# A mixture-of-experts loop on one Trainium2 core: rows taken from a table in memory, weight splits on one engine, a branch hint moved

## The chip, the core and the metric

The kernel runs on one core of a Trainium2 chip, in one launch. Its engines are TensorE (PE, matmuls into PSUM), VectorE (DVE), ScalarE (ACT), GpSimd (POOL) and SyncE (SP). Here SP issues nearly all plain DMA transfers and POOL the indirect ones, which gather or scatter rows by a list of row numbers in SBUF. Each engine runs its own list of instructions in order, and engines wait for each other on semaphores. The metric is the device time of one execution in microseconds; lower is better.

## What is computed

One layer of a hybrid decoder over 1024 tokens of width 1024, in float32: a LayerNorm, one wide projection, three token mixers (gated DeltaNet, mLSTM, latent attention), their gated merge and output projection, a LayerNorm, a mixture of 16 experts with top-2 routing inside one of four groups, and a last LayerNorm. The change touches the experts:

```python
def routed_experts(x, router_w, router_bias, w1, w3, w2):
    expert, weight = route(x_flat, router_w, router_bias)
    ...
    def expert_ffn(args):
        xb, e = args
        return (jax.nn.silu(xb @ w1[e]) * (xb @ w3[e])) @ w2[e]
    ...
    out = jnp.zeros((n_tok, d), x.dtype).at[row_tok].add((y_rows * row_w[:, None]).astype(x.dtype))
```

So each expert needs the numbers of the tokens sent to it, their weights, and their rows of x.

## The kernel before

**Stages.** The first 1382 us are everything up to the second LayerNorm. Then the router scores all tokens (`route_choose`, `route_weights`), and `experts` runs the 16 experts one after another. Each token's place within its expert's list stands in `posx` (tokens on partitions, one column an expert).

**How an expert's rows are found.** `mark(e)` makes eight one-hot tiles on VectorE (L1437) that compare `posx` with 0 to 255. `find(e)` multiplies them with `aux` (token number, a valid flag, the weight in three bfloat16 parts) on TensorE (L1455), which leaves the list by place; `found(e)` spreads the further places over quarters of rows (four matmuls, L1461) and makes, in some dozen small VectorE operations (L1464 to L1480), `idx` (which row to gather, which row of the result to add to) and the weights `wsl`. Both have four buffers.

**One expert.** Places 0 to 127 are a full block: `fetch(e)` gathers the 128 rows of 4 KB into `xg` (POOL, L1489); `turn_a` transposes them on TensorE (`pxg`, L1505) and splits them into a high and a low part (`xgH` on ScalarE, `xgL` on VectorE); `layer1` multiplies with w1 and w3 in eight chunks c (`ph`, L1535), `act` makes silu times gate (`mhh`), `turn2` transposes (`phT`, L1510) and `layer2` multiplies with w2 in four chunks (`py`). The result is scaled by the weights on ScalarE (`mo`, L1743) and added to its rows of `x1r` in memory by an indirect DMA of POOL (L1494). Places from 128 on are up to four parts of 32, each under a branch on the expert's count; they gather quarter rows into `xm`, run in `part_x`, `part_1`, `part_act`, `part_h`, `part_2`, `part_y` on the tile `bank`, and end in `mom` and up to four more adds. The branch code stands at the helper line L1659; `ahead` places a hint that names a later branch of TensorE.

**Weights.** Each weight tile (128 x 1024) is loaded raw by SP (L1574), then split: ScalarE copies a high part (L1590), and the low part, raw minus high, is a subtraction (L1591) on VectorE, or on POOL for tiles with i % 6 in (3, 5), four of an expert's twelve. Every matmul is done three times with these parts. `Weights.step` makes up to three splits after a chunk and starts loads until twelve raw tiles are ahead, as buffers come free.

**Order.** The loop has passes e = 0 to 14 of twelve chunks. In pass e chunks 0 to 7 are the first layer of expert e, chunks 8 to 11 the second layer of expert e-1. After each chunk come the entries of the table `AT` (`AT0` in pass 0): `(9, "fetch", 2)` means that after chunk 9 of pass e, `fetch(e+2)` is issued. PE, DVE and ACT keep this written order; SP's and POOL's are arranged by the tile scheduler. A tile with n buffers is written again only when all readers of the n-th one before are done; where they are transfers, when these have landed. The last two experts have a list of their own (`last_two`).

Of the kernel before, what the change touches and what calls it, by code (L numbers as in the profile page):

```python
# [11 lines left out]
I32 = mybir.dt.int32  # L12
# [1306 lines left out]
def route_consts(k, pool):  # L1319
# [29 lines left out]
    for q in range(4):  # L1349
# [69 lines left out]
def route_weights(k, pool, lo, hi):  # L1419

    nc = k.nc
    n = hi - lo
    wt = pool.tile([P, n, NE], F32, name="wt", bufs=1)
    ws = pool.tile([P, n], F32, name="ws", bufs=1)
    nc.vector.tensor_tensor(wt, k.sc[:, lo:hi], k.selb[:, lo:hi], OP.mult)
    nc.vector.tensor_reduce(ws, wt, AX.X, OP.add)
    nc.vector.reciprocal(ws, ws)
    nc.vector.tensor_tensor(wt, wt, bc(ws, NE), OP.mult)
    for i in range(3):
        nc.vector.tensor_copy(k.aux[:, lo:hi, :, 3 + i], wt)  # L1430
        if i < 2:
            nc.vector.tensor_sub(wt, wt, k.aux[:, lo:hi, :, 3 + i])

# [10 lines left out]
def places(k, oh, aux, cols=(0, 6), parts=False):  # L1444
# [198 lines left out]
def experts(k, ws):  # L1643
# [23 lines left out]
    def ahead(e, name, m=0):  # L1667

        tc.mark_branch_hint_location(f"{name}_{e}_{m}", hint=count_of(e, nc.tensor) > P + 32 * m, engines=[ENG.PE])

    def find(e, cols=(0, 6)):
        a = A.setdefault(e, Block())
        a.places = places(k, k.oh, lambda b: k.aux[:, b, e], cols, True)
        next(a.places)

    def found(e):
        a = A[e]
        idx, w = next(a.places)
        if w is not None:
            a.w = w  # L1680
        if idx is not None:
            a.idx, a.row = idx[:, 0], idx[:, 1]

    def fetch(e, both=True):
# [3 lines left out]
        if not hasattr(a, "xg"):  # L1688
            a.xg = k.rc.tile([P, D], F32, name="xg")
            gather(k, a.xg, k.x1, a.idx[:, 0:1])  # L1690
        if both:
            per_part(e, lambda m: gather(k, k.xm[:, m], xq, a.idx[:, 1 + m:2 + m]), nc.gpsimd)

    with tc.manual_schedule(engines=MANUAL | {ENG.Pool}):
        find(0, (0, 3))
        found(0)
        fetch(0)
        route_weights(k, k.rc, 0, NB)
    with tc.tile_pool(name="moe", bufs=2) as pool:
# [34 lines left out]
        def layer2(e, c, add=True):  # L1734
# [586 lines left out]
def hybrid_kernel(ctx, tc, aps, out):  # L2321
# [80 lines left out]
```

## Time and profile before

| | us |
|---|---|
| median of 3 runs | 1921.68 (1918.59 to 1933.87) |
| the profiled execution | 1925.09 |
| its span, first to last instruction | 1923.3 |
| up to the routing | 0 to 1382 |
| the routing | 1382 to 1400 |
| the loop over experts | 1400 to 1867.7 |
| the last expert's end and the last LayerNorm | 1867.7 to 1923.3 |

The profile is of one execution by the hardware profiler. Engines' busy times are sums of their instructions' durations; the line numbers are those of the kernel before. PEq and SPq are the engines' sequencers: time on a branch or in issuing a transfer. PEclk is TensorE's granted clock, 1.00 being full speed.

### The profile page before, as it was taken

The numbers are of one execution on the slowest core, as the hardware profiler recorded it, in microseconds if no ns is written. First come the engines' busy times: TensorE is split into PE (matmuls) and PEld (weight loads), VectorE is DVE, ScalarE is ACT, GpSimd is POOL, SyncE is SP. The second block draws the span as 40 slices with busy tenths as digits, with TensorE's granted clock in tenths as the row PEclk, the third lists the DMA queues.
The fourth block names the chain that finished last, engine by engine and source line by source line (L and its number), as shares of the span: only waits on it lengthen the run. The fifth ranks groups of instructions, "written<-read, shape, count | busy, mean of one in ns | idle before, by whom it ended". The sixth has DMA issues, their size and how long they took to land. (4 is left out here: it accounts for less than half of the span.)

```text
span 1923.3 us, 29628 instructions
## 1 busy us (share of the span) xinstructions
PE 1723.6 (90%) x10830; PEld 1441.2 (75%) x10830; DVE 1225.7 (64%) x2279; ACT 703.1 (37%) x1166; POOL 603.1 (31%) x503
## 2 busy tenths in 40 slices
PE   6996999999999999999999899998488888878782
PEld 5974988899998888888777688898356655656551
DVE  7699645554555343444476747736776758999886
ACT  6321322212212213345344522213154446666563
POOL 3186021113311104532100200005334555545455
PEclk9998999999999999999999999999698989898996
DMA  5232533233432234533200355352556768898755
GB/s 172 88 110 109 182 100 118 90 119 90 118 90 87 84 111 127 159 116 121 69 17 18 106 192 190 124 190 110 216 191 196 214 190 288 291 293 271 244 151 201
DMA packets 210661, 286.34 MB, mean 149 GB/s; under 512 B 33358, under 2 KB 138824, under 8 KB 210472
## 3 DMA queue, kind: packets, MB, share of 16 engines
q1 hardware_dynamic: 202312, 258.87, 40.5%
q0 software_dynamic: 8160, 24.91, 5.3%
q8 instruction: 124, 2.03, 0.4%
q14 instruction: 65, 0.53, 0.1%
HBM read 214.64 MB, written 69.07 MB: 148 GB/s over the span
## 5 line engine op out<-in xcount | busy, mean ns | idle before, releaser
L365 PE MATMUL psp<-xH,wh 128*128 128x512 f32 x704 | 286.0, 406 | 18.7 <-ACT ci L519 18.7
L366 PE MATMUL psp<-xL,wh 128*128 128x512 f32 x704 | 275.6, 391 | 4.0 <-POOL ci L514 2.2
L367 PE MATMUL psp<-xH,wl 128*128 128x512 f32 x704 | 276.9, 393 | 0.0
L365 PEld LDWEIGHTS psp<-xH,wh 128*128 128x128 f32 x704 | 133.2, 189 | 44.3 <-ACT ci L519 20.0
L365 PE MATMUL psp<-wh,xH 128*128 128x256 f32 (+1 forms) x576 | 166.1, 288 | 0.0
L367 PE MATMUL psp<-wh,xL 128*128 128x256 f32 (+1 forms) x576 | 162.9, 283 | 0.0
L366 PE MATMUL psp<-wl,xH 128*128 128x256 f32 (+1 forms) x576 | 162.9, 283 | 0.0
L366 PEld LDWEIGHTS psp<-xL,wh 128*128 128x128 f32 x704 | 133.2, 189 | 30.8 <-POOL ci L514 2.6
L367 PEld LDWEIGHTS psp<-xH,wl 128*128 128x128 f32 x704 | 132.6, 188 | 29.4
L365 PEld LDWEIGHTS psp<-wh,xH 128*128 128x128 f32 x576 | 110.9, 193 | 0.2
L366 PEld LDWEIGHTS psp<-wl,xH 128*128 128x128 f32 x576 | 110.9, 193 | 0.1
L367 PEld LDWEIGHTS psp<-wh,xL 128*128 128x128 f32 x576 | 110.8, 192 | 0.0
L351 DVE TENSOR_TENSOR wl<-wr,wh 128x1024 fp32r<-128x1024 f32 (+1 forms) x62 | 81.9, 1339 | 41.9 <-ACT wh L350 29.9
L1535 PE MATMUL ph<-wl,xgH 128*128 128x512 f32 x274 | 89.9, 436 | 10.8 <-PEq L1659 6.9
L350 ACT ACTIVATE wh<-wr 128x1024 fp32r<-128x1024 f32 (+1 forms) x62 | 64.0, 1048 | 64.6 <-PE psp L366 42.8
L365 PE MATMUL pbr<-yH,brh 128*128 128x512 f32 x192 | 75.5, 393 | 0.5 <-DMA ya<-ay 0.5
L366 PE MATMUL pbr<-yL,brh 128*128 128x512 f32 x192 | 75.6, 393 | 0.0
L367 PE MATMUL pbr<-yH,brl 128*128 128x512 f32 x192 | 75.3, 392 | 0.0
L365 PE MATMUL pwo<-woh,mH 128*128 128x256 f32 x256 | 75.2, 294 | 0.0
L366 PE MATMUL pwo<-wol,mH 128*128 128x256 f32 x256 | 73.6, 287 | 0.0
L367 PE MATMUL pwo<-woh,mL 128*128 128x256 f32 x256 | 73.5, 287 | 0.0
L1535 PEld LDWEIGHTS ph<-wl,xgH 128*128 128x128 f32 x274 | 53.4, 206 | 26.4 <-issue 9.7
(844 smaller groups left out, 4433.6 us busy)
## 6 DMA issues: line engine op xcount, KB each, us to landing
wl<-in_moe_w_dram SPq DMA_DIRECT2D x126, 256.0 KB, 5.3
wr<-in_w_in_dram SPq DMA_DIRECT2D x60, 512.0 KB, 5.0
xs<-in_moe_w_dram SPq DMA_DIRECT2D x82, 256.0 KB, 3.7
wl<-in_moe_w_dram SPq DMA_DIRECT2D x34, 512.0 KB, 8.2
gates<-gt SPq DMA_DIRECT2D x24, 512.0 KB, 2.8
mgt<-gates SPq DMA_DIRECT2D x48, 256.0 KB, 2.9
we<-in_moe_w_dram SPq DMA_DIRECT2D x48, 256.0 KB, 5.3
we<-in_moe_w_dram SPq DMA_DIRECT2D x18, 512.0 KB, 4.7
```

Source lines behind the costliest of these rows:

```text
L350: k.nc.scalar.activation(h, raw, AF.Copy)
L351: k.nc.vector.tensor_sub(l, raw, h)
L365: k.nc.tensor.matmul(out, aH, bH, start=start, stop=False)
L366: k.nc.tensor.matmul(out, aH, bL, start=False, stop=False)
L367: k.nc.tensor.matmul(out, aL, bH, start=False, stop=stop)
L1535: k.nc.tensor.matmul(ps, xL if p == 2 else xH, wl if p == 1 else wh, start=first and p == 0, stop=last and p == 2)
```

## The change

For experts 2 to 15 the search is replaced by a table in memory, `k.table`, with 16 x 256 entries of four words: token number, row of the result, weight, unused. POOL and SP fill it with blank entries early on; after the routing each token writes its two entries (`route_table`: 18 VectorE operations and 16 indirect DMAs of POOL). `look(e)` reads an expert's entries by five small SP transfers, 2 KB each: `tab0` for the first 128 places, and four for `tabq`, the quarters; `looked(e)` makes the row numbers of the quarters in one VectorE operation (`tabi`). All three have three buffers. Experts 0 and 1 are still searched for. All splits of weights go to VectorE. The hint `ahead_1` for the next expert's first-layer parts moves from chunk 8 to chunk 3 (chunk 2 in pass 0); two other branches of TensorE, `part_h` and `part_x`, now stand between it and its branch.

```diff
@@ route_consts
+    blank = k.xm[:, 1].bitcast(I32)[:, :NE * CAPA // P * 4].rearrange("p (j c) -> p j c", c=4)
+    nc.gpsimd.memset(blank, 0)
+    nc.gpsimd.iota(blank[:, :, 1], pattern=[[0, NE * CAPA // P]], base=T, channel_multiplier=1)
+    nc.sync.dma_start(k.table[0:NE * CAPA].rearrange("(j p) c -> p j c", p=P), blank)
...
+def route_table(k, pool, wt):
...
+    for b in range(NB):
+        for i in range(2):
+            d = nc.gpsimd.indirect_dma_start(out=k.table, out_offset=bass.IndirectOffsetOnAxis(ap=to[:, i, b:b + 1], axis=0),
+                                             in_=entry[:, i, b], in_offset=None)
...
+            k.written.append(d.ins)
@@ places
-        idx = k.rc.tile([P, 2, 1 + NM], I32, name="idx", bufs=4)[:, :, :n]
-        f, r = (k.rc.tile([P, 1 + NM], F32, name=t, bufs=2)[:, :n] for t in ("fsl", "rsl"))
+        idx = k.rc.tile([P, 2, 1 + NM], I32, name="idx", bufs=2)[:, :, :n]
+        f, r = (k.rc.tile([P, 1 + NM], F32, name=t, bufs=1)[:, :n] for t in ("fsl", "rsl"))
...
-        w = k.rc.tile([P, 1 + NM], F32, name="wsl", bufs=4)[:, :n]
+        w = k.rc.tile([P, 1 + NM], F32, name="wsl", bufs=2)[:, :n]
@@ Weights.split
-POOL_SPLIT = (3, 5)
...
-            (nc.gpsimd if i % 6 in POOL_SPLIT else nc.vector).tensor_tensor(l, raw, h, OP.subtract)
+            nc.vector.tensor_tensor(l, raw, h, OP.subtract)
@@ experts
+    def look(e):
+        a = A.setdefault(e, Block())
+        lo = CAPA * e + P
+        a.t0 = k.rc.tile([P, 4], I32, name="tab0", bufs=3)
+        a.tq = k.rc.tile([P, NM, 4], I32, name="tabq", bufs=3)
+        ds = [nc.sync.dma_start(a.t0, k.table[CAPA * e:lo])]
+        for q in range(4):
+            ds.append(nc.sync.dma_start(a.tq[32 * q:32 * q + 32],
+                                        k.table[lo:lo + CAPA - P].rearrange("(m r) c -> r m c", r=32)))
...
+    def looked(e):
+        a = A[e]
+        iq = k.rc.tile([P, 2, NM], I32, name="tabi", bufs=3)
+        nc.vector.tensor_scalar(iq, a.tq[:, :, 0:2].rearrange("p m c -> p c m"), 4.0, k.rowadd[:, 1:2], op0=OP.mult,
+                                op1=OP.add)
+        a.i0, a.r0, a.w0 = a.t0[:, 0:1], a.t0[:, 1:2], a.t0[:, 2:3].bitcast(F32)
+        a.iq, a.rq, a.wq = iq[:, 0], iq[:, 1], a.tq[:, :, 2].bitcast(F32)
...
-                    nc.scalar.activation(o[:, i * DE:i * DE + DE], a.y[i], AF.Copy, scale=a.w[:, 0:1])
-                add_rows(k, k.x1r, a.row[:, 0:1], o)
+                    nc.scalar.activation(o[:, i * DE:i * DE + DE], a.y[i], AF.Copy, scale=a.w0)
+                add_rows(k, k.x1r, a.r0, o)
...
             events(AT0, 0, -1)
+            route_table(k, k.rc, wt)
             turn_a(0)
...
 AT0 = ((-1, "mark", 1), (0, "find", 1), (1, "part_x", 0), (1, "ahead_1", 0), (2, "found", 1), (2, "fetch", 1),
-       (2, "part_1", 0), (3, "mark", 2), (5, "part_act", 0), (5, "find", 2), (6, "part_h", 0),
-       (6, "found", 2), (7, "act", 0), (7, "turn_a", 1), (7, "part_x", 1), (8, "ahead_1", 1), (9, "mark", 3), (9, "fetch", 2))
+       (2, "part_1", 0), (2, "ahead_1", 1), (5, "part_act", 0), (5, "look", 2), (6, "part_h", 0),
+       (7, "act", 0), (7, "turn_a", 1), (7, "part_x", 1), (7, "looked", 2), (9, "fetch", 2))
 AT = ((0, "part_1", 0), (0, "turn2", -1), (0, "ahead_2", -1), (1, "part_act", 0), (3, "turn_a", 1), (3, "part_2", -1),
-      (4, "part_h", 0), (4, "find", 2), (5, "part_y", -1), (6, "found", 2), (7, "act", 0),
-      (8, "part_x", 1), (8, "ahead_1", 1), (9, "mark", 3), (9, "fetch", 2))
+      (3, "ahead_1", 1), (4, "part_h", 0), (4, "look", 2), (5, "part_y", -1), (6, "looked", 2), (7, "act", 0),
+      (8, "part_x", 1), (9, "fetch", 2))
```

**SP, the read of `tab0` for expert 8, in pass 6**, with the semaphores that each row waits for (DMAHW: SP's own transfers by lane; DMASW: landings of POOL's indirect transfers; Activation, DVE, PE: instructions of those engines). `wl_...`, `xs1_...` and `we_3...` are raw weight tiles of later experts:

```order
L1618 DMA wl_9_16737<-in_moe_w1_dram 128x512 [waits DMAHW5_49,PE_49,Activation_49]
L1618 DMA wl_9_16737<-in_moe_w3_dram 128x512 [waits DMAHW6_49]
L1720 DMA tab0_16398<-table_76 128x4 [waits DMASW6_49,DMAHW7_49,DMASW1_49,Activation_49]
L1618 DMA xs1_16750<-in_moe_w1_dram 128x512 [waits DMAHW0_49,DVE_49,PE_49]
L1618 DMA xs1_16750<-in_moe_w3_dram 128x512 [waits DMAHW1_49]
L1618 DMA we_3_16897<-in_moe_w2_dram 128x1024 [waits DMAHW2_49,PE_49]
```

The read is new. Its two DMASW waits are, in the program, the landings of `xg` and of `x1r<-mo` of expert 5, and its Activation wait is the second half of that expert's `mo`; the DMAHW wait is its lane. The weight loads stand behind it on SP.

**POOL, before: the gather of an expert's rows and what stands around it**, at the end of a pass (ISA rows count semaphores up where a part doesn't run):

```order
L1659 ISA
L1659 UNCONDITIONAL_BRANCH
L1489 DMA xg<-x_58,idx 128x1024
L1659 UNCONDITIONAL_BRANCH
L1659 COMPARE_AND_BRANCH x4
L1489 DMA xm<-x_58,idx 128x256
```

**POOL, after: the same place**, in pass 7; `tab_15422` is `tab0` of expert 6, whose second layer has just ended, and `tab_16886` that of expert 9, whose rows are gathered:

```order
L1703 UNCONDITIONAL_BRANCH
L1703 ISA
L1703 UNCONDITIONAL_BRANCH
L1539 DMA x1r<-mo,tab_15422 1152x1024
L1703 UNCONDITIONAL_BRANCH
L1534 DMA xg<-x_58,tab_16886 128x1024
L1703 UNCONDITIONAL_BRANCH x2
L1703 COMPARE_AND_BRANCH
```

The gather stood ahead of the `xm` gathers and of the add `x1r<-mo`; now it stands behind them.

**VectorE, after: chunks 5 and 6 of the same pass 6**; the L1635 rows are splits, `mom_16417` is expert 5's, `tabi_16439` expert 8's:

```order
L1635 TENSOR_TENSOR wl_16_16406<-we_6_15921,we_5_16405 128x1024 [waits DMAHW0_49,Activation_49]
L1867 TENSOR_TENSOR mom_16417<-bank_13074,tabq_14935 128x1024 [waits PE_49]
L1635 TENSOR_TENSOR wl_0_16428<-wl_8_15943,wl_11_16427 128x1024 [waits Activation_49]
L1703 UNCONDITIONAL_BRANCH x2
L1733 TENSOR_SCALAR tabi_16439<-tabq_16399,rowadd_11477 128x8 [waits DMAHW2_49,DMAHW3_49,DMASW7_49,DMAHW4_49,DMASW6_49,DMAHW5_49,DMASW1_49,DMASW0_49]
L1635 TENSOR_TENSOR wl_14_16442<-wl_3_15957,xs0_16441 128x1024 [waits Activation_49]
```

The `tabi` row is new, one split behind `mom`. Its DMAHW waits are the four `tabq` reads and its DMASW waits the four adds of `mom_16417`, or what counts for them where a part doesn't run.

## Rows read from the trace of the kernel before

**Rows 1.** The page's first lines: busy us, share of the span, instructions
```profile
span 1923.3 us, 29628 instructions
PE 1723.6 (90%) x10830; PEld 1441.2 (75%) x10830; DVE 1225.7 (64%) x2279; ACT 703.1 (37%) x1166; POOL 603.1 (31%) x503
```

**Rows 2.** Windows: us, busy us of each engine, PEclk, DMA share; last: L1591 alone
```profile
1400.00:1602.00 202.00, 172.24 (x1446) 119.93 (x1447) 139.17 (x227) 96.31 (x119) 94.32 (x48) 0.92 0.67 209
1602.00:1844.40 242.40, 198.47 (x1017) 145.71 (x1016) 223.84 (x300) 153.25 (x190) 126.34 (x59) 0.94 0.86 276
1602.00:1844.40 242.40, 135.90 (x72) 97.58 (x38) 0.94 0.86 276
```

**Rows 3.** The same, T to pxg or pxg to T: passes 4, 6, 6, 9, 14, 14
```profile
1531.30:1544.80 13.50, 11.23 (x94) 7.81 (x93) 12.37 (x9) 5.97 (x8) 10.36 (x6) 0.87 0.64 201
1602.00:1610.60 8.60, 6.55 (x29) 4.45 (x29) 8.40 (x9) 5.92 (x8) 7.80 (x4) 1.00 0.65 215
1610.60:1627.70 17.10, 15.74 (x110) 11.20 (x109) 16.72 (x30) 11.16 (x14) 7.80 (x4) 1.00 1.01 314
1683.10:1691.00 7.90, 6.35 (x29) 4.56 (x29) 7.90 (x12) 5.93 (x8) 6.18 (x4) 1.00 0.82 257
1814.70:1829.90 15.20, 11.63 (x94) 7.24 (x93) 8.86 (x7) 5.96 (x8) 4.84 (x3) 0.89 0.61 168
1829.90:1844.40 14.50, 13.28 (x60) 9.97 (x58) 14.40 (x11) 11.10 (x14) 8.68 (x4) 1.00 0.76 288
```

**Rows 4.** Timeline of pass 9's end and pass 10's start: start us, us, engine, line
```profile
1702.85 1.00 POOL L1489 DMA_INDIRECT xg<-x,idx  x1 [2.58 <-DVE wsl L1478]
1705.12 2.41 POOL L1591 TENSOR_TENSOR wl<-we,wl 128x1024 fp32r<-128x1024 f32 x1 [1.26 <-DMA wl<-in_moe_w_dram]
1705.54 3.07 DVE L1591 TENSOR_TENSOR we<-wl,we 128x1024 fp32r<-128x1024 f32 x1
1707.11 0.63 PE L1535 MATMUL py<-wl,mhL 128*128 128x512 f32 x2
1707.54 1.27 ACT L1743 ACTIVATE mo<-py,wsl 128x512 f32<-128x512 f32 x2 [0.61 <-PE py L1535]
1715.98 1.04 PE L1505 MATMUL pxg<-ident,xg 128*128 128x128 f32 x8
```

**Rows 5.** Tile mo in 1602 to 1845 us: its add x1r<-mo on POOL
```profile
DMA to landing us min/median/max: 6.2/7.6/12.2
```

**Rows 6.** Tile xg in 1400 to 1870 us: its gather
```profile
DMA to landing us min/median/max: 4.2/5.5/7.8
```

**Rows 7.** DMA issues: out<-in, count, KB each, median us to landing
```profile
gT<-i16T SPq DMA_DIRECT2D x8, 32.0 KB, 1.7
cs<-cq SPq DMA_DIRECT2D x8, 64.0 KB, 3.9
x1r<-mom,idx POOLq DMA_INDIRECT x11, 6.1
```

**Rows 8.** Line 1591 in 1400 to 1870 us: ns min/median/max
```profile
L1591 DVE TENSOR_TENSOR wl<-wl,wl x16: 1208/1226/3430, 1422.7 to 1869.8; 128x1024 fp32r<-128x1024 f32 x16
```

**Rows 9.** Groups of the search in 1602 to 1845 us: busy us, mean ns | idle before
```profile
L1437 DVE TENSOR_SCALAR oh<-iob,posx 128x256 bf16<-128x256 bf16 x60 | 29.9, 588 | 0.0
L1464 DVE COPY slb<-psl 128x30 f32<-128x30 f32 x8 | 1.4, 176 | 0.0
L1455 PE MATMUL psl<-aux,oh 128*128 128x6 bf16 x128 | 4.6, 165 | 5.5 <-DVE xgL L1517 3.4 <-issue 1.5
L1461 PE MATMUL psl<-spl,spread 128*128 128x6 bf16 x32 | 2.0, 168 | 0.2 <-DVE spl L1458 0.2
```

**Rows 10.** Waits of TensorE in 1602 to 1845 us: total us, times, longest
```profile
PE phT L1510 <- PEq L1659: 17.2, 6, 4.0
```

**Rows 11.** The loop's start: a wait of TensorE in 1382 to 1425; POOL's timeline
```profile
PE pxg L1505 <- DMA xg<-x,idx: 6.7, 2, 4.2
1410.89 1.06 POOL L1489 DMA_INDIRECT xg<-x,idx  x1 [0.30 <-DMA xs<-in_moe_w_dram]
```

More of the change, by code (lines that the diff above doesn't have):

```diff
@@ L1354, in route_consts @@
                                    op1=OP.add)
+    k.past = pc
+    nc.vector.tensor_scalar(pc, pc, float(NE * CAPA + 1), None, op0=OP.add)
     k.spread = pool.tile([P, NM, 4, 32], BF, name="spread")
@@ L1428, in route_weights @@
     nc.vector.tensor_tensor(wt, wt, bc(ws, NE), OP.mult)
+    rest = wt
     for i in range(3):
-        nc.vector.tensor_copy(k.aux[:, lo:hi, :, 3 + i], wt)
+        nc.vector.tensor_copy(k.aux[:, lo:hi, :, 3 + i], rest)
         if i < 2:
-            nc.vector.tensor_sub(wt, wt, k.aux[:, lo:hi, :, 3 + i])
+            part, rest = rest, k.sc[:, lo:hi]
+            nc.vector.tensor_sub(rest, part, k.aux[:, lo:hi, :, 3 + i])
+    return wt
+def route_table(k, pool, wt):
+    nc, tc = k.nc, k.tc
+    v, eq, first, entry = k.logit, k.sc, k.rbias, k.trib.bitcast(I32).rearrange("p (i b c) -> p i b c", i=2, c=4)
+    small = k.cum.rearrange("p b e -> p (b e)").bitcast(F32)[:, :4 * 2 * NB].rearrange("p (n i b) -> p n i b", i=2, b=NB)
+    at, w, far, to = (small[:, i] for i in range(4))
+    to = to.bitcast(I32)
+    nc.gpsimd.iota(first, pattern=[[CAPA, NE]], base=0, channel_multiplier=0, allow_small_or_imprecise_dtypes=True)
+    nc.gpsimd.iota(entry, pattern=[[0, 2], [P, NB], [0, 4]], base=0, channel_multiplier=1)
+    big = 2.0 * NE * CAPA
+    nc.vector.tensor_tensor(v, k.selb, bh(first, NB), OP.mult)
+    nc.vector.tensor_add(v, v, k.posx)
+    nc.vector.tensor_scalar(eq, k.posx, float(CAPA), big, op0=OP.is_gt, op1=OP.mult)
+    nc.vector.tensor_add(v, v, eq)
+    nc.vector.tensor_reduce(at[:, 0], v, AX.X, OP.max)
+    nc.vector.tensor_reduce(at[:, 1], v, AX.X, OP.add)
+    nc.vector.tensor_sub(at[:, 1], at[:, 1], at[:, 0])
+    for i in range(2):
+        nc.vector.tensor_tensor(eq, v, bc(at[:, i], NE), OP.is_equal)
+        nc.vector.tensor_mul(eq, eq, wt)
+        nc.vector.tensor_reduce(w[:, i], eq, AX.X, OP.add)
+    nc.vector.tensor_scalar(entry[:, :, :, 2].bitcast(F32), w, 0.5 / ALPHA, None, op0=OP.mult)
+    nc.vector.tensor_scalar(far, at, -1.0, k.past, op0=OP.mult, op1=OP.add)
+    nc.vector.tensor_scalar(w, at, big, None, op0=OP.is_ge)
+    nc.vector.tensor_mul(far, far, w)
+    nc.vector.scalar_tensor_tensor(to, at, -1.0, far, op0=OP.add, op1=OP.add)
+    for b in range(NB):
+        for i in range(2):
+            d = nc.gpsimd.indirect_dma_start(out=k.table, out_offset=bass.IndirectOffsetOnAxis(ap=to[:, i, b:b + 1], axis=0),
+                                             in_=entry[:, i, b], in_offset=None)
+            tc.declare_no_dep(d.ins, group="table", reason="no two tokens have the same entry")
+            tc.add_to_no_dep_group("table", d.ins)
+            k.written.append(d.ins)
@@ L1669, in ahead @@
         tc.mark_branch_hint_location(f"{name}_{e}_{m}", hint=count_of(e, nc.tensor) > P + 32 * m, engines=[ENG.PE])
+    def look(e):
[7 more added lines that the diff above has]
+                                        k.table[lo:lo + CAPA - P].rearrange("(m r) c -> r m c", r=32)))
+        for d in ds:
+            for w in k.written:
+                tc.add_manual_dep(d.ins, w.name, mybir.DependencyInfo(mybir.DependencyClass.Sync,
+                                                                      mybir.DependencyReason.DATA),
+                                  reason="the table is whole")
+    def looked(e):
[5 more added lines that the diff above has]
+        a.iq, a.rq, a.wq = iq[:, 0], iq[:, 1], a.tq[:, :, 2].bitcast(F32)
     def find(e, cols=(0, 6)):
@@ L1679, in found @@
         if w is not None:
-            a.w = w
+            a.w0, a.wq = w[:, 0:1], w[:, 1:]
         if idx is not None:
-            a.idx, a.row = idx[:, 0], idx[:, 1]
+            a.i0, a.iq, a.r0, a.rq = idx[:, 0, 0:1], idx[:, 0, 1:], idx[:, 1, 0:1], idx[:, 1, 1:]
     def fetch(e, both=True):
@@ L1689, in fetch @@
             a.xg = k.rc.tile([P, D], F32, name="xg")
-            gather(k, a.xg, k.x1, a.idx[:, 0:1])
+            gather(k, a.xg, k.x1, a.i0)
         if both:
-            per_part(e, lambda m: gather(k, k.xm[:, m], xq, a.idx[:, 1 + m:2 + m]), nc.gpsimd)
+            per_part(e, lambda m: gather(k, k.xm[:, m], xq, a.iq[:, m:m + 1]), nc.gpsimd)
     with tc.manual_schedule(engines=MANUAL | {ENG.Pool}):
@@ L1697, in experts @@
         fetch(0)
-        route_weights(k, k.rc, 0, NB)
+        wt = route_weights(k, k.rc, 0, NB)
     with tc.tile_pool(name="moe", bufs=2) as pool:
@@ L1799, in part_y @@
             o = pool.tile([P, NM, 256], F32, name="mom", bufs=1)
-            nc.vector.tensor_tensor(o, bank[:, :, 256:], bc(a.w[:, 1:], 256), OP.mult)
-            per_part(e, lambda m: add_rows(k, rq, a.row[:, 1 + m:2 + m], o[:, m]), nc.gpsimd)
+            nc.vector.tensor_tensor(o, bank[:, :, 256:], bc(a.wq, 256), OP.mult)
+            per_part(e, lambda m: add_rows(k, rq, a.rq[:, m:m + 1], o[:, m]), nc.gpsimd)
         def last_two(d, e):
             a, norm = A[e], Norm(k)
-            z, row = k.rest = ws.spare(True), a.row[:, 0:1]
+            z, row = k.rest = ws.spare(True), a.r0
             t = pool.tile([P, D], F32, name="mo")
@@ L1820, in whole @@
                     h = z[:, i * DE:i * DE + DE]
-                    nc.vector.scalar_tensor_tensor(h, a.y[i], a.w[:, 0:1], h, op0=OP.mult, op1=OP.add)
+                    nc.vector.scalar_tensor_tensor(h, a.y[i], a.w0, h, op0=OP.mult, op1=OP.add)
                     nc.vector.bn_stats(bs[:, 6 * i:6 * i + 6], h)
@@ L1832, in last_two @@
                    "turn2": lambda: turn2(e), "layer2": lambda: mul(layer2, e, False),
-                   "consts": lambda: norm.consts(ws.spare), "gather": lambda: gather(k, z, k.x1r, a.idx[:, 0:1]), "whole": whole}
+                   "consts": lambda: norm.consts(ws.spare), "gather": lambda: gather(k, z, k.x1r, a.i0), "whole": whole}
             for name in LAST.split():
@@ L1840, in last_two @@
             k.norm = norm
-        fns = {"mark": lambda n: mark(k, n), "turn_a": turn_a, "find": find, "found": found, "fetch": fetch, "part_x": part_x,
+        fns = {"mark": lambda n: mark(k, n), "turn_a": turn_a, "find": find, "found": found, "look": look, "looked": looked, "fetch": fetch, "part_x": part_x,
                "part_1": part_1, "part_act": part_act, "part_h": part_h, "part_2": part_2, "part_y": part_y, "act": act,
@@ L2348, in hybrid_kernel @@
     k.x1r = scratch("x1r", [T + P, D])
+    k.table = dp.tile([NE * CAPA + P, 4], I32, name="table")
+    k.written = []
     k.cp = ent(tc.tile_pool(name="cp_", bufs=1))
```

## Prediction

> **What bounds the kernel now.** The page's first lines show TensorE busy for 90% of a span of 1923.3 us [rows 1]; that is an average over stages, so the windows come next. Of the change, only the stretch from the routing (about 1382 us) on can move: before it, both versions issue the same work. In the loop over experts I cut the windows at the last `py` matmul of each pass, the moment T at which the previous expert's second layer is done. In 1602.0 to 1844.4 us, the nine passes e = 6 to 14, whose experts run few or no parts, the picture differs from the page: in 242.4 us TensorE is busy 198.5, VectorE 223.8 (92%), the DMA engines 0.86 of the time [rows 2]. A pass takes 26.9 us and TensorE has 22.1 us of work in it.
>
> Inside a pass the point to watch is `pxg`, the transpose of the next expert's gathered rows, at c = 3. From T to `pxg` take 7.9 to 15.2 us over the nine passes (100.0 in all), from `pxg` to the next T mostly 14.5 to 17.1 (142.4 in all); the first and last passes and the shortest way to `pxg` stand in [rows 3]. (The windows of those nine passes add up to the 242.4 of [rows 2].) The gather of `xg` never ends last there: in the pass of [rows 4] it was issued at 1702.85 us and needed at 1716.0.
>
> **The change, step by step.**
>
> *Search removed.* For experts 2 to 15 go eight one-hot operations on VectorE (29.9 us for 60, 4.0 a pass) and 12 small ones (0.18 each, 2.1), with 20 small matmuls: 6.6 us for eight experts, 0.8 a pass [rows 9].
>
> *All splits on VectorE.* 38 splits on POOL took 97.6 us in the nine passes and 72 on VectorE 135.9, 1.89 us each [rows 2]; alone one takes 1.22 us (the median), beside a POOL split 3.07 [rows 4, 8]. Afterwards 12 a pass at 1.22 are 14.6 us instead of 15.1. VectorE falls from 24.9 us to about 24.9 - 4.0 - 2.1 - 0.5 = 18.3 us a pass. It would no longer press, and the four more splits cost nothing, since they are covered by the 12.7 us that it is then free in a pass of 31. (The Trainium skill, "SBUF — State Buffer", section "Who interferes with whom", says that a VectorE instruction with two SBUF inputs contends with a GpSimd instruction that reads SBUF; the 3.07 us beside 1.22 agree. It speaks for this part.)
>
> *The hint earlier.* The first layer's branch misses cost TensorE 17.2 us in six waits at `phT`, just behind T [rows 10]. All of it lies between T and `pxg`; whether `pxg` still waits for that is decided by the next step.
>
> *The table's reads: a new serial chain.* On SP five reads an expert join the weight loads. `tab0` has three buffers, but four experts are alive. The read of `tab0(e+2)` in pass e (from e = 3 on) overwrites the entry of expert e-1, whose last readers stand at the end of the same pass: the scaling of its result into `mo` on ScalarE and the landing of the add `x1r<-mo`, which takes its row numbers there. SP's order shows the wait, with the weight loads queued behind it, and POOL's shows `xg` behind that add; before, `idx` and `wsl` had four buffers and `xg` was issued some 5 us ahead of T. So the chain now starts at T:
> T to the end of `mo`: 1707.74 to 1708.81, 1.1 us [rows 4]; add, issue to landing: 7.6 (6.2 to 12.2) [rows 5]; `tab0`, a 2 KB read: the nearest row is the small `gT` transfer, 1.7, with 3.9 as upper bound from `cs<-cq` [rows 7]; `xg`, issue to landing: 5.5 (4.2 to 7.8) [rows 6]. That sums to 15.9 us; I take 16. Bounds: all shortest 13.2; with 3.9 for the read and a `xg` of 7.8, 20.4. TensorE reaches c = 3 in 7.9 us when nothing stops it, so it would wait about 8 us for `xg` in every pass without parts. (The Trainium skill, "SBUF — State Buffer", section "The DMA setup-cost knee", gives every transfer a fixed 2 us however few its bytes, which speaks against five small reads on a chain; by it the read is 2.0 instead of 1.7 and the sum 3 us higher.)
>
> From `pxg` to T the mean was 142.4 / 9 = 15.8; less 0.8 for the search it is 15.0, so a pass takes 31.0 instead of 26.9. Lower bound of this half: TensorE's busy time in it, 13.3 in the last pass [rows 3], less 0.8, 12.5; upper: 17.5, about the longest before, where late weights or TensorE's granted clock eat the relief (after a wait behind T it stood at 0.89 up to `pxg` in the last pass, against 1.00 behind it [rows 3]). Nine passes: 9 x 4.1 = +37. In pass 4 parts already stretch T to `pxg` to 13.5 [rows 3], in pass 5 beyond 16: +2.5 and 0. The hint gives nothing here: `pxg` waits for the chain, which does not pass through that branch.
>
> *`tabq` and `tabi`.* They have three buffers too, and the readers that hold them are expert e-1's `mom`, on VectorE at c = 5, and its adds on POOL. `tabi` stands on VectorE two rows behind `mom`, with the splits queued behind it. With parts the adds land 6.1 us after issue [rows 7], so VectorE stands some 6 to 8 us, in about four passes; VectorE was free for 63 of 202 us in 1400 to 1602 [rows 2], which covers most. I take +1 each, +4; all uncovered it would be 4 x 7 = +28. Without parts it waits only for the four `tabq` reads, about 1.7 us behind four issues.
>
> *The start.* 16 scatters on POOL at the 1.06 us of a gather's row [rows 11] are 17 us, ahead of `xg(1)`, which went out at 1410.9 and was needed by 1418.8. The two POOL splits removed there and POOL's idle time cover most; I take +4 (0 to 15). The 18 VectorE operations of the table (18 x 0.28 at most, 5 us) run beside the 4.2 us that TensorE waits for `xg(0)` [rows 11]: 0. The first memset and its transfer lie in the front, where POOL has room.
>
> *Relief in passes 0 to 5.* Six searches at 0.8 = -5, and -0.5 each from VectorE and POOL: -8.
>
> Sum against the profiled execution (1925.1): +37 + 2.5 + 4 + 4 - 8 = 1964.6. That execution lay 3.4 us above the median of the runs shown, so **1961**.
>
> **Rivals.**
> *A, faster: the read is early enough.* If `xg` lands within 8 us of T, the pass falls to its floors: TensorE 21.3 us, VectorE 18.3, transfers 276 GB/s x 26.9 us = 7.4 MB, which at the 314 GB/s of [rows 3] take 23.6. With 23 us a pass, 9 x -3.9 = -35, with -8 and +4: 1925 - 39 - 3.4 = 1883. VectorE's 92% speaks for it; against it, the shortest add landing alone is 6.2 and the shortest chain 13.2.
> *B, even.* Chain and second half both near the lower bounds (13.2 + 14.0 = 27.2): 9 x +0.3 = +3, the other terms -4: 1921. For it: with SP standing at `tab0`, fewer weight transfers run beside the add and the gather, and landings shorten.
> *C, slower still: weights starve.* On SP the weight loads stand behind `tab0`. If SP waits there until T + 8.7 and the DMA engines then need 23.6 us for a pass's weights, less some 5 already under way, a pass is at least 27, and where that eats the lead of the loads the second half grows to 18: 34 us a pass, 9 x 7.1 = +64, total about 1988. Against: twelve raw tiles are loaded ahead, a full pass.
> *D, the hint is lost.* Two other branches now stand between it and its branch. Its price is at most the 17.2 us of A, none in the forecast; it moves A to about 1900.
>
> **How the numbers follow.** The likeliest, `xg` late and the second half little changed, gets 0.50, its own range 1941 to 1985. A with D 0.17, B 0.21, C 0.12. I call a change of 1% (19 us) about what a measurement of this kernel can tell from none: faster (below 1902.5) 0.17, same 0.21, slower 0.62. The range, 1900 to 1990, leaves out most of A and the top of C.
>
> **What would show it.** Right: a wait of TensorE `pxg <- DMA xg` of 6 to 10 us in passes 6 to 14, SP's queue waiting at the table's line for `x1r<-mo`, `xg` issued 9 to 12 us after T, passes near 31 us. VectorE's splits at 1.22 with no long ones, and idle time ahead of `tabi`. Wrong: `xg` issued before T, or passes of 23 us; then the buffers do not bind as read from the order. If passes are long but the wait is at `ph` for splits or weights, C holds. If passes 0 to 5 lose more than 10 us, the scatters or `tabi` were undersized.

## The result, and the profile after

The changed kernel takes 2083.3 us in the median (2080.6 to 2088.9), 1.0835 times the time before (four runs, median 1922.3; 95% interval of the ratio 1.0794 to 1.0875): 8.4% slower, where 2.0% was forecast. The profiled execution took 2080.6 us. TensorE is busy for 84% of the span, after 90% [rows 1]:

```profile
span 2078.8 us, 28852 instructions
PE 1748.4 (84%) x10550; PEld 1454.4 (70%) x10550; DVE 1152.3 (55%) x2096; ACT 705.2 (34%) x1166; POOL 465.0 (22%) x459
```

Up to the routing both traces agree. From there the 155.5 us by which the span grew divide as follows, cut at the last `py` of a pass (T):

| stretch | before | after | more | forecast |
|---|---|---|---|---|
| up to the end of pass 3 | 1531.3 | 1543.5 | +12.2 | near 0 |
| pass 4 | 34.4 | 56.5 | +22.1 | +3 |
| pass 5 | 36.3 | 38.3 | +2.0 | 0 |
| passes 6 to 13 | 212.7 | 317.5 | +104.8 | +33 |
| pass 14 and the end | 108.6 | 123.0 | +14.4 | +4 |

Windows of the changed kernel (columns as in [rows 2]): the eight passes 6 to 13, then pass 10 from T to `pxg` and from `pxg` to T, which answer to [rows 3]:

```profile
1638.30:1955.80 317.50, 190.36 (x707) 137.21 (x706) 158.24 (x169) 137.55 (x169) 33.07 (x19) 0.76 0.62 187
1792.50:1813.80 21.30, 6.72 (x29) 4.58 (x28) 11.14 (x12) 5.99 (x8) 3.51 (x2) 0.73 0.72 228
1813.80:1831.70 17.90, 16.51 (x57) 12.15 (x57) 8.60 (x10) 11.25 (x14) 0.00 (x0) 0.75 0.47 141
```

A pass takes 39.7 us instead of 26.6. VectorE, busy 92% of such a stretch before, is now busy 50% (158.2 of 317.5), the DMA engines 0.62 instead of 0.86, and TensorE itself 60% (190.4): no engine is near its limit. TensorE's three largest waits in the eight passes (total us, times, longest):

```profile
PE pxg L1550 <- DMA xg<-x,tab: 98.8, 8, 16.0
PE ph L1580 <- ACT xgH L1561: 6.6, 6, 1.2
PE phT L1555 <- PEq L1703: 6.5, 3, 2.4
```

So the wait for `xg`, zero there before, is 98.8 us in eight passes. SP's queue names its cause at the table's line (SP waits longer in all for weight buffers that TensorE has still to free, 139.6 us, but in each of the eight passes it is the add's landing that ends the wait ahead of `tab0`):

```profile
SPq L1720 <- DMA x1r<-mo,tab: 40.9, 8, 7.7
```

Pass 10 by timelines (start us, us, engine, line), ScalarE, POOL, SP and TensorE:

```profile
1792.35 1.26 ACT L1810 ACTIVATE mo<-py,tab 128x512 f32<-128x512 f32 x2
```
```profile
1793.89 2.51 POOL L1539 DMA_INDIRECT x1r<-mo,tab  x1 [26.63 <-ACT mo L1810]
1804.92 1.00 POOL L1534 DMA_INDIRECT xg<-x,tab  x1 [8.52 <-DMA tab<-table]
```
```profile
1802.53 0.33 SPq L1720 DMA_DIRECT2D tab<-table  x1
1802.96 0.85 SPq L1618 DMA_DIRECT2D xs<-in_moe_w_dram  x2
```
```profile
1813.81 1.94 PE L1550 MATMUL pxg<-ident,xg 128*128 128x128 f32 x8 [13.79 <-DMA xg<-x,tab]
```

T is 1792.5. `mo` ends at 1793.6, the add is issued at 1793.9, and only when it has landed does SP read `tab0`, at 1802.5. `xg` goes out at 1804.9 and TensorE begins `pxg` at 1813.8, after 13.8 us of waiting. Right behind `tab0` SP issues the weight loads that stood behind it.

### The profile page after: what moved, and what is told of

The parts are those of the page before. It is cut to its first block, busy times and chain, and to the rows that moved or that the text cites. A ratio compares the mean times of both kernels' runs of the same rounds, so it can differ in the third digit from the quotient of the medians.

```text
span 2078.8 us, 28852 instructions
## 1 busy us (share of the span) xinstructions
PE 1748.4 (84%) x10550; PEld 1454.4 (70%) x10550; DVE 1152.3 (55%) x2096; ACT 705.2 (34%) x1166; POOL 465.0 (22%) x459
## 5 line engine op out<-in xcount | busy, mean ns | idle before, releaser
L1580 PE MATMUL ph<-wl,xgH 128*128 128x512 f32 x274 | 102.5, 483 | 34.8 <-issue 20.1
L1550 PE MATMUL pxg<-ident,xg 128*128 128x128 f32 x128 | 26.4, 375 | 122.8 <-DMA xg<-x,tab 114.3
L1550 PEld LDWEIGHTS pxg<-ident,xg 128*128 128x128 f32 x128 | 21.5, 195 | 128.1 <-issue 127.7
L1580 PEld LDWEIGHTS ph<-wl,xgH 128*128 128x128 f32 x274 | 60.3, 232 | 59.9 <-issue 33.9
L1562 DVE TENSOR_TENSOR xgL<-pxg,xgH 128x512 fp32r<-128x512 f32 x32 | 21.6, 689 | 117.4 <-ACT xgH L1561 117.2
L1561 ACT ACTIVATE xgH<-pxg 128x512 fp32r<-128x512 f32 x32 | 18.7, 597 | 170.9 <-PE pxg L1550 170.7
```

The source lines that it names most:

```text
L1550: k.nc.tensor.transpose(px[c // 4][:, c % 4], xg[:, c * P:c * P + P], k.ident)
L1561: k.nc.scalar.activation(bl.xH[:, s], px[q], AF.Copy)
L1562: k.nc.vector.tensor_sub(bl.xL[:, s], px[q], bl.xH[:, s])
L1580: k.nc.tensor.matmul(ps, xL if p == 2 else xH, wl if p == 1 else wh, start=first and p == 0, stop=last and p == 2)
```

## Experiments

Where two experiments are compared, it is by their ratios to the kernel before, each with its 95% interval.

**A buffer for the fourth expert.** `all_four` gives the three tiles a fourth buffer; `tab0_four` and `quarters_four` do one half each.

```diff
-    sb = k.rc.tile([P, 1 + NM, 6], F32, name="slb", bufs=2)[:, :n]
+    sb = k.rc.tile([P, 1 + NM, 6], F32, name="slb", bufs=1)[:, :n]
...
-        a.t0 = k.rc.tile([P, 4], I32, name="tab0", bufs=3)
-        a.tq = k.rc.tile([P, NM, 4], I32, name="tabq", bufs=3)
+        a.t0 = k.rc.tile([P, 4], I32, name="tab0", bufs=4)
+        a.tq = k.rc.tile([P, NM, 4], I32, name="tabq", bufs=4)
...
-        iq = k.rc.tile([P, 2, NM], I32, name="tabi", bufs=3)
+        iq = k.rc.tile([P, 2, NM], I32, name="tabi", bufs=4)
```

> The changed kernel with four buffers instead of three for tab0, tabq and tabi (and one instead of two for slb, which only experts 0 and 1 still use, to make room). Theory 1, the fourth expert has no buffer and the chain add, table read, gather is the loss: TensorE's wait for xg falls from 114 us to under 10, passes 6 to 14 fall from 39.7 us to about 24, the time to 1870 to 1900 us. Theory 2, the loss lies in the other parts (16 scatters, five more reads on SP, all splits on VectorE): it stays above 2040 us.

> The changed kernel with four buffers for tab0 alone. Theory 1a, the chain through tab0 is the loss of passes 6 to 14 and tabi's wait that of passes 3 to 5: the waits for xg go, tabi's waits for the adds of mom (28.5 us in four) stay, the time is 1900 to 1945 us. Theory 1b, tabi, which holds the splits behind it on VectorE, is as large: above 1980 us.

> The changed kernel with four buffers for tabq and tabi, three for tab0 (slb one). Theory 1a: passes 6 to 14 stay at about 39 us, pass 4 loses some 15 us of its 56, the time is 2040 to 2065 us. Theory 1b: below 1990 us.

Measured: `all_four` 1918.8 us, ratio 0.9955 (0.9925 to 0.9984); `tab0_four` 1982.0, 1.0293 (1.0244 to 1.0341); `quarters_four` 2048.8, 1.0654 (1.0610 to 1.0708). The buffers are the whole loss and a little more: 8.8% of the time, some 169 us, lies between the changed kernel and `all_four`. The three for `tab0` cost 7.0% by themselves (`quarters_four` less `all_four`, 134 us), those of the quarters 3.4% by themselves (`tab0_four` less `all_four`, 65 us), so that `tab0_four` lies well above the 1945 us of its theory 1a; on top of the chain through `tab0` the quarters cost 1.8% (the changed kernel less `quarters_four`, 35 us). Together they cost less than the sum of 199 us; that they delay the same passes would explain it and was not tested. `all_four` stayed above its expected 1870 to 1900 us, though its passes 6 to 13 fell to 24.0 us as expected. There the DMA engines are nearly always busy (columns as above: DMA share 0.94, 317 GB/s), but TensorE's largest waits are neither for `xg` nor for splits, and its work (161.6 us) and all its waits (27.0) fill 188.6 of the 191.6 us; that the transfers bind now is not shown. The window, and the two largest waits in it:

```profile
1604.30:1795.90 191.60, 161.61 (x708) 122.61 (x707) 157.01 (x170) 136.31 (x169) 30.01 (x20) 0.96 0.94 317
```
```profile
PE phT L1555 <- PEq L1703: 10.5, 3, 3.8
PE ph L1580 <- ACT xgH L1561: 6.6, 6, 1.2
```

**Who holds whom in the 19.9 us from the add's issue to `pxg` (pass 10).** `tab0_by_pool` lets POOL issue the read, so that no weight load stands behind it.

```diff
-        ds = [nc.sync.dma_start(a.t0, k.table[CAPA * e:lo])]
+        ds = [nc.gpsimd.dma_start(a.t0, k.table[CAPA * e:lo])]
```

> The changed kernel with tab0 read by a transfer that POOL issues instead of SP; three buffers as they are. The chain add, read, gather stays, but no weight loads stand behind the read. If the weights that SP held back and then issued all at once just ahead of the gather are why the gather took 8 to 9 us to land: it lands in 5 to 6, T to pxg falls from 21.5 to about 18 us, the time to about 2050 us. If they are not: 2075 to 2090 us, T to pxg as before.

Measured: 2073.8 us, 1.0765 (1.0713 to 1.0817), 0.7% less than the changed kernel, with intervals that overlap; some 2050 us were expected. Pass 10 here, POOL and TensorE, T at 1807.9:

```profile
1809.28 2.53 POOL L1539 DMA_INDIRECT x1r<-mo,tab  x1 [22.72 <-ACT mo L1810]
1819.33 0.60 POOL L1720 DMA_DIRECT2D tab<-table  x1 [7.52 <-DMA x1r<-mo,tab]
1824.71 0.99 POOL L1534 DMA_INDIRECT xg<-x,tab  x1 [4.79 <-DMA tab<-table]
```
```profile
1829.47 1.94 PE L1550 MATMUL pxg<-ident,xg 128*128 128x128 f32 x8 [14.08 <-DMA xg<-x,tab]
```

The gather takes 4.8 us instead of 8.9; over passes 6 to 13 the mean from its issue to `pxg` is 4.4 against 8.8. That half of the expectation held: loads which were held and then released just ahead of the gather double its time. But from the read's issue on POOL to the gather's 5.6 us pass in the mean instead of 2.5, and the add needs 9.4 until the read goes out instead of 8.9, so T to `pxg` is 20.8 us in the mean instead of 21.6. That the longer read is due to the weights beside it and not to POOL's issue is borne out by the last such read of this run: issued at 1973.18 with the DMA engines at 0.06, it took 2.7 us up to the gather at 1975.91, against 5.4 in pass 10 with the DMA engines at 0.61. The weights' traffic delays whichever small transfer it meets.

**Why `pxg` to T takes 18 us.** After the wait TensorE's granted clock is at its lower level (0.50 of 2.4 GHz, so 1.2). The changed kernel, pass 10, in four windows:

```profile
1806.00:1813.80 7.80, 0.00 (x0) 0.03 (x1) 0.00 (x0) 0.00 (x0) 0.00 (x0) 0.50 0.73 267
1813.80:1820.00 6.20, 4.96 (x15) 3.49 (x15) 2.61 (x3) 2.26 (x4) 0.00 (x0) 0.50 0.03 5
1820.00:1825.00 5.00, 5.00 (x17) 3.98 (x18) 3.49 (x3) 3.31 (x4) 0.00 (x0) 0.73 0.68 213
1825.00:1831.70 6.70, 6.55 (x28) 4.69 (x26) 2.50 (x4) 5.67 (x7) 0.00 (x0) 1.00 0.73 213
```

It stood at 0.50 for the last 7.8 us of idling and for the first 6.2 us after it. `quarters_four_warm` puts 48 matmuls into the wait of `quarters_four`, in passes 4 to 13.

```diff
+            if 5 <= e < NE - 1:
+                b = A[e - 1]
+                for _ in range(48):
+                    nc.tensor.matmul(px[0], b.xL[:, 0], b.xH[:, :4], start=True, stop=True)
             turn_x(k, px, a.xg)
```

> The kernel quarters_four with 48 extra matmuls of 128x512 on TensorE ahead of pxg of experts 5 to 14, which fill about 11 us of its wait for xg; their results are overwritten. If TensorE's granted clock (0.50 from the end of the wait on, in the changed kernel) is why pxg to T takes 17.4 us instead of the 15.0 of the forecast: the clock stays at 1.00, pxg to T falls to about 15 us, the time by some 20 us to about 2028 us. If late weights or splits are the reason: pxg to T stays at 17 us and the time at 2040 to 2060 us.

Measured: 2048.3 us, 1.0671 (1.0613 to 1.0730), equal to `quarters_four`. The passes tell more than the total. `quarters_four`, passes 6 to 13 together and one second half:

```profile
1623.50:1922.50 299.00, 175.42 (x708) 132.47 (x707) 159.08 (x170) 137.01 (x169) 26.55 (x19) 0.78 0.64 200
1792.60:1809.50 16.90, 15.42 (x57) 11.84 (x58) 11.65 (x13) 11.17 (x14) 0.00 (x0) 0.79 0.50 156
```

`quarters_four_warm`, the second halves of passes 9 and 10:

```profile
1771.20:1785.30 14.10, 12.72 (x58) 9.89 (x57) 11.06 (x13) 11.07 (x14) 0.00 (x0) 1.00 0.58 184
1805.80:1822.10 16.30, 14.92 (x57) 11.46 (x58) 11.14 (x13) 11.14 (x14) 0.00 (x0) 0.81 0.48 158
```

In pass 9 the extra matmuls ran right up to `pxg`: clock 1.00, second half 14.1 us. In pass 10 they did not reach that far: 0.81 and 16.3. Passes 7, 9 and 11, of the first kind, took 33.9 to 35.1 us, the other five 36.8 to 38.1, as in `quarters_four` (36.0 to 38.6). In those three the second half fell from 17.9, 16.4 and 16.9 us to 14.2, 14.1 and 14.3, so the lower clock after the wait is worth some 2.3 to 3.6 us a pass. The total hides it: passes 6 to 13 took 290.4 us instead of 299.0, but passes 4 and 5, where `xg` is not late by so much and the 48 matmuls stand in the way, 95.0 instead of 86.2. The profiled execution was a further 9.3 us behind at the end of pass 3, where no matmul has been added yet.

**The quarters' buffers.** With `tab0` cured, TensorE waits at `py` for splits (first two rows, `tab0_four`, passes 6 to 13), and VectorE at `tabi` (whole loop):

```profile
PE py L1580 <- DVE wl L1635: 14.4, 4, 6.4
PE py L1580 <- DVE we L1635: 12.0, 3, 5.8
```
```profile
DVE tabi L1733 <- DMA tabq<-table: 47.0, 7, 9.4
DVE tabi L1733 <- DMA x1r<-mom,tabi: 30.3, 4, 15.8
```

`tab0_four_looked10` makes `tabi` later and, with it, issues the gathers later (after chunk 11 instead of 9), `tab0_four_tabq_pool` reads `tabq` by POOL, `tab0_four_both` does both.

```diff
-            ds.append(nc.sync.dma_start(a.tq[32 * q:32 * q + 32],
+            ds.append(nc.gpsimd.dma_start(a.tq[32 * q:32 * q + 32],
...
-      (3, "ahead_1", 1), (4, "part_h", 0), (4, "look", 2), (5, "part_y", -1), (6, "looked", 2), (7, "act", 0),
-      (8, "part_x", 1), (9, "fetch", 2))
+      (3, "ahead_1", 1), (4, "part_h", 0), (4, "look", 2), (5, "part_y", -1), (7, "act", 0),
+      (8, "part_x", 1), (10, "looked", 2), (11, "fetch", 2))
```

> The kernel tab0_four with tabi made after chunk 10 instead of 6 (and the gathers after chunk 11), three buffers for the quarters as they are. If the 63 us by which tab0_four is above all_four come from the splits that stand behind tabi on VectorE while it waits: nearly all of it goes, 1920 to 1940 us. If they come from the weight loads that stand behind tabq on SP while it waits for mom: it stays above 1965 us.

> The kernel tab0_four with the four tabq reads issued by POOL instead of SP, tabi after chunk 6 as in the change. No weight load stands behind tabq any more; the splits still stand behind tabi on VectorE. If SP's hold on the weight loads is the price of the three quarter buffers: 1920 to 1945 us. If the splits behind tabi are: 1970 us or more, with TensorE waiting at py for splits.

> The same with tabi after chunk 10: neither weight loads nor the next pass's first splits are held. If the two holds together are the 63 us between tab0_four and all_four: 1915 to 1940 us. If it stays above 1960 us, the three buffers cost in a third place: the gathers of xm and xg, which POOL issues behind the reads.

Measured, in this order: 1967.5 us, 1.0249 (1.0203 to 1.0295); 1993.8 us, 1.0350 (1.0303 to 1.0397); 1920.3 us, 0.9979 (0.9957 to 1.0002). Each edit alone gives 0.4% at most, within the intervals, both together 3.1%, all but the last few us of the price. With `tabi` later, SP still stands at `tabq` until `mom` has read the old entries, and `xg` comes late behind that (first row SP's queue, second TensorE, passes 6 to 12):

```profile
SPq L1722 <- DVE mom L1867: 53.3, 7, 9.3
```
```profile
PE pxg L1550 <- DMA xg<-x,tab: 25.7, 4, 6.8
```

The later gathers alone do not explain it: in `tab0_four_both` they stand as late, and TensorE has no wait for `xg` in passes 6 to 13.

With `tabq` on POOL, VectorE still stands at `tabi`:

```profile
DVE tabi L1733 <- DMA tabq<-table: 56.4, 8, 9.3
```

Either hold suffices to be late; an experiment that removes one alone would have acquitted both.

**The splits.** `four_poolsplit` puts four of twelve splits of `all_four` back on POOL; `before_dve` has all splits on VectorE in the kernel before.

```diff
-            nc.vector.tensor_tensor(l, raw, h, OP.subtract)
+            (nc.gpsimd if i % 6 in (3, 5) else nc.vector).tensor_tensor(l, raw, h, OP.subtract)
```

> The kernel all_four with four of twelve splits back on POOL. If the splits on VectorE alone, without contention, brought passes 6 to 13 from 26.6 to 23.9 us, these rise to about 26 and the time to about 1935 us. If the removed search did it: passes stay at 24 us, within 5 us of all_four.

> The kernel before with all splits on VectorE and nothing else. VectorE then has 12 splits of 1.22 us with the search's 6.1 us beside them, 24.9 - 0.5 = 24.4 us a pass: if the contention with POOL was the loss, 1900 to 1912 us; if VectorE's load is what binds, 1915 to 1930 us.

Measured: `four_poolsplit` 1937.2 us, 1.0092 (1.0064 to 1.0119); `before_dve` 1914.4 us, 0.9956 (0.9939 to 0.9973). With the search gone the move is worth 1.4%; alone, with the search still on VectorE, 0.4%.

**The hint.** `four_hint8` is `all_four` with the hint at chunk 8; `before_hint3` is the kernel before with it at chunk 3 (2 in pass 0).

```diff
...
-      (3, "ahead_1", 1), (4, "part_h", 0), (4, "look", 2), (5, "part_y", -1), (6, "looked", 2), (7, "act", 0),
-      (8, "part_x", 1), (9, "fetch", 2))
+      (4, "part_h", 0), (4, "look", 2), (5, "part_y", -1), (6, "looked", 2), (7, "act", 0),
+      (8, "part_x", 1), (8, "ahead_1", 1), (9, "fetch", 2))
```

> The kernel all_four with the hint back at chunk 8, as before the change. If the hint at chunk 3 is lost to the two branches that stand between, or stalls TensorE (ph waits 19.4 us on nothing visible, behind part_2, where the hint stands): those waits go and the time falls to 1900 to 1912 us. If the early hint saves the waits at phT: they rise from 20.5 us to about 27, and the time by 5 to 10 us.

> The kernel before with the hint at chunk 3 (2 in pass 0) and nothing else. If the early hint saves first-layer branch misses: the waits at phT fall from 26 to about 10 us in the loop and the time to 1905 to 1915 us. If it only moves them (four_hint8 was equal to all_four): new waits at ph that the profile names issue, and 1918 to 1930 us.

Measured: `four_hint8` 1910.0 us, 0.9948 (0.9924 to 0.9971), not to be told from `all_four`; `before_hint3` 1926.2 us, 1.0028 (1.0004 to 1.0051). TensorE's waits, `all_four` with the early hint, then `four_hint8`, 1400 to 1800 us, and `before_hint3`, 1400 to 1845:

```profile
PE ph L1580 <- issue: 19.4, 8, 5.4
PE phT L1555 <- PEq L1703: 16.0, 8, 3.8
PE ph L1580 <- PEq L1703: 10.5, 10, 4.6
```
```profile
PE phT L1555 <- PEq L1703: 30.7, 13, 4.1
PE ph L1580 <- PEq L1703: 25.6, 14, 11.4
```
```profile
PE phT L1510 <- PEq L1659: 14.4, 8, 3.2
PE ph L1535 <- issue: 11.3, 6, 4.4
```

The early hint does halve the waits at `phT` (30.7 to 16.0). In their place come waits at `ph` for nothing that the profile shows, in passes with parts behind `part_2`, where the hint now stands: 19.4 us in `all_four`, 11.3 in `before_hint3`, against 1.7 and none with the late hint. All of TensorE's waits in these windows add up to 64.3 us in `all_four` and 66.1 in `four_hint8`, 77.6 in `before_hint3` and 72.5 in the kernel before: the sum moves little, and the time does not fall.

**The start, and what can be had.** `late_table` writes the table after chunk 2 of pass 0 and reads it from chunk 9 on. `late_hint8` is that with the hint at chunk 8. `best_pool` is `four_hint8` with `tabq` by POOL and `tabi` after chunk 10; `best_pool_late` adds the late table; `best_sp` is `best_pool` with `tabq` left on SP. They are put together from the edits above and this one:

```diff
-            route_table(k, k.rc, wt)
...
-AT0 = ((-1, "mark", 1), (0, "find", 1), (1, "part_x", 0), (1, "ahead_1", 0), (2, "found", 1), (2, "fetch", 1),
-       (2, "part_1", 0), (2, "ahead_1", 1), (5, "part_act", 0), (5, "look", 2), (6, "part_h", 0),
-       (7, "act", 0), (7, "turn_a", 1), (7, "part_x", 1), (7, "looked", 2), (9, "fetch", 2))
+AT0 = ((-1, "mark", 1), (0, "find", 1), (1, "part_x", 0), (1, "ahead_1", 0), (2, "found", 1), (2, "fetch", 1), (2, "table", 0),
+       (2, "part_1", 0), (2, "ahead_1", 1), (5, "part_act", 0), (6, "part_h", 0),
+       (7, "act", 0), (7, "turn_a", 1), (7, "part_x", 1), (9, "look", 2), (10, "looked", 2), (11, "fetch", 2))
```

> The kernel all_four with the table written after chunk 2 of pass 0, behind the gather of expert 1's rows instead of ahead of it, and read from chunk 9 on. If the 16 scatters ahead of that gather cost the 10 us by which pxg of expert 1 came later (1428.6 instead of 1418.8), TensorE's wait there falls from 6.7 us to about 2 and the time to 1905 to 1912 us. If that work is late anyway: 1915 to 1925 us.

> The best of what was found, together: four buffers for tab0, tabq and tabi, the table written behind the gather of expert 1's rows, the hint at chunk 8. If the parts add: late_table gained nothing over all_four, four_hint8 nothing, so 1908 to 1918 us; if the start's 10 us had only been hidden by chance: about 1903 us.

> The kernel four_hint8 (four buffers, hint at chunk 8) with tabq read by POOL and tabi after chunk 10, as in tab0_four_both, whose passes 6 to 13 took 22.8 us against 24.0 in all_four. If that 1.2 us a pass comes from SP without the small reads: about 1900 us; if tab0_four_both only caught up what it had lost in passes 4 and 5: 1908 to 1915 us.

> The same with the table written behind the gather of expert 1's rows. 1893 to 1903 us if both count; equal to best_pool within 4 us if passes 1 to 5 are bound elsewhere.

> The kernel four_hint8 with tabi after chunk 10 and tabq still on SP: tells which of the two edits of best_pool counts. Equal to best_pool if it is tabi's place, equal to four_hint8 (1910 us) if it is the queue.

| kernel | us | ratio to before |
|---|---|---|
| `late_table` | 1914.2 | 0.9960 (0.9944 to 0.9977) |
| `late_hint8` | 1911.1 | 0.9955 (0.9928 to 0.9982) |
| `best_pool` | 1912.2 | 0.9920 (0.9887 to 0.9953) |
| `best_pool_late` | 1905.0 | 0.9875 (0.9832 to 0.9918) |
| `best_sp` | 1928.4 | 1.0012 (0.9990 to 1.0034) |

In `late_table` `pxg` of expert 1 comes at 1417.4 us instead of 1428.6 in `all_four`, as expected, but the total gains nothing: the intervals overlap. `best_pool_late`, 1.25% below the kernel before, is the fastest that was found, though its interval overlaps that of `best_pool`. `best_sp` was expected to equal `best_pool` or `four_hint8` and is slower than both: the small reads' queue counts when `tabi` stands late (0.9% above `best_pool`), and the late `tabi` by itself is a loss (0.6% above `four_hint8`). Whether the late table is worth anything in `best_pool_late` is not shown.

## Why the prediction was wrong

The direction, the place and the mechanism were as forecast: three buffers for four experts, so that `xg` waits for the previous expert's add and the table's read. The sizes of its terms were not.

*"That sums to 15.9 us; I take 16."* Measured in passes 6 to 13: 21.6 from T to `pxg` in the mean. In pass 10 the add took 8.6 us until the read went out (7.6 in [rows 5]), read and hand-over 2.4 (1.7 in [rows 7]), the gather 8.9 up to `pxg` (5.5 in [rows 6]). The gather is the largest miss. Its median came from the kernel before, where no read on SP held the loads back; here SP releases them just ahead of the gather, and `tab0_by_pool` shows the 4.4 us that it takes with most of them gone. The upper end was set at 20.4, too low by 1.2: it kept the add at its median, though the longest in [rows 5] was 12.2.

*"It is 15.0."* The second half took 18.1. TensorE's busy time in it, 16.5 us in pass 10, is what the lower clock stretches from some 12.7 (`quarters_four_warm`, pass 9). The forecast named the clock among the bounds and put no term to it. Rival C had 18 for this half, but for another reason, starved weights, and met it by luck: TensorE's waits for splits are 7.7 us in all eight passes together, and with TensorE kept at work the half fell to 14.1. Both misses together, 31.0 against 39.7 a pass, are 70 of the 122 us by which the forecast fell short.

*"I take +1 each, +4."* The quarters were the term most undersized: 65 us by themselves, 35 on top of the chain. Two things were missing. The forecast said that VectorE's free time covers its wait at `tabi`, but a wait in an ordered queue is not covered by idle time that comes later: the splits behind it are the next ones that TensorE needs. And `tabq` holds the weight loads on SP, which the forecast named for `tab0` alone. With parts, the adds of `mom` wait for each other's landing. Pass 4, POOL, VectorE and a wait of TensorE:

```profile
1581.56 2.30 POOL L1539 DMA_INDIRECT x1r<-mom,tabi  x1 [22.74 <-DVE mom L1867]
1588.75 1.55 POOL L1539 DMA_INDIRECT x1r<-mom,tabi  x1 [4.89 <-DMA x1r<-mom,tabi]
1592.65 1.55 POOL L1539 DMA_INDIRECT x1r<-mom,tabi  x1 [2.34 <-DMA x1r<-mom,tabi]
```
```profile
1596.56 0.23 DVE L1733 TENSOR_SCALAR tabi<-tabq,rowadd 128x8 int32<-128x8 int32 x1 [14.14 <-DMA x1r<-mom,tabi]
```
```profile
PE py L1580 <- DVE xs L1635: 10.4, 1, 10.4
```

VectorE stood 14.1 us, twice the 6 to 8 forecast, and TensorE 10.4 behind it.

*"I take +4 (0 to 15)" for the start.* The 16 scatters took from 1397.8 to 1422.0, 24 us instead of 17, with 0.3 us between each two and several of 1.5 to 2.0:

```profile
1397.83 1.00 POOL L1473 DMA_INDIRECT table<-trib,cum  x1 [8.37 <-DVE xgL L1562]
...
1421.05 0.97 POOL L1473 DMA_INDIRECT table<-trib,cum  x1 [0.30 <-issue]
1424.89 0.94 POOL L1534 DMA_INDIRECT xg<-x,idx  x1 [0.30 <-issue]
```

`xg` of expert 1 went out at 1424.9 instead of 1410.9 [rows 11], and its `pxg` at 1429.6 instead of 1418.8: +10.8. Inside the range given, above the value taken.

*Relief.* Right in size, not in place. VectorE's splits are uniform now:

```profile
L1635 DVE TENSOR_TENSOR wl<-wl,wl x11: 1212/1218/1226, 1670.3 to 1939.5; 128x1024 fp32r<-128x1024 f32 x11
```

and without the new waits a pass falls to 24.0 us, where rival A said 23 (less than its own 23.6 for the transfers). (That the 3 us splits are gone with POOL's agrees with the Trainium skill, "SBUF — State Buffer", section "Who interferes with whom".) But A's 1883 us was not reached with four buffers. In `all_four` passes 6 to 13 gained 21.1 us, where A said 31; pass 5 ends at 1604.3 against 1602.0, and pass 14 and the end take 114.7 us against 108.6. `pxg` of expert 1 came 9.8 us late there, so passes 0 to 5 made up 7.5 of it, near the forecast's -8. Yet in `late_table`, with that start back at 1417.4, pass 5 still ends at 1600.3: whether the -8 is there stays open. Of the hint it said that it gives nothing here. That held, and even where no chain covers it, it gives nothing. (The Trainium skill's 2 us for a small transfer, "SBUF — State Buffer", section "The DMA setup-cost knee", and the row of 1.7 cannot be told apart here: read and hand-over together took 2.4.)

*The range* ended at 1990 because each term's upper bound stood alone. The bound of the quarters, +28, and of the chain, 20.4 and 17.5, were there; taken together with the start's 15 they give 1925 + 9 x 11 + 28 + 15 - 8 - 3 = 2056, most of the way. Bounds of separate terms have to be added where one cause moves them together, as too few buffers do.

## What to carry to other kernels

Count the buffers of a tile by its last reader, a landing of an indirect transfer included, and by how many users are alive: one buffer too few in three tiles of 16 to 64 bytes a partition cost 169 us here. When a transfer that waits is put on a queue, everything behind it waits too, and what it releases meets the next small transfer. Price such a chain with what will run beside it, and add TensorE's slower second half to a long wait ahead of it.

## What the runs showed of the hardware

- After 13.8 us without work TensorE ran at granted clock 0.50 for its next 6 us, and eight transposes took 1.94 us instead of 1.04 [rows 4].
- The same gather of 128 rows needed 4.4 us up to its use in `tab0_by_pool` and 8.8 in the changed kernel, behind released weight loads (means of passes 6 to 13; in pass 10 the DMA engines stood at 0.35 and 0.76). From the issue of a 2 KB read to that of the gather that needs it 2.4 us passed when SP issued it ahead of the loads, 5.4 when POOL did beside them (pass 10 of each), and 2.7 when POOL did with the DMA engines at 0.06.
- With an earlier hint TensorE's branch waits at `phT` fell from 26.1 to 14.4 us in the kernel before, and 11.3 us of waits for nothing that the profile shows came up at `ph` on the same engine.
